# Encoder trunk on one core: the second FFN product in five groups of weight pairs, with its other work placed by a clock kept at build time

## The chip, the cores and the metric

The kernel runs on one core of a Trainium2 chip. The metric is the device time of one execution in microseconds (us), as the median of several runs. A profile is one further execution, taken by the hardware profiler. Engines are named as in the profile: PE (TensorE, matmuls), PEld (its weight loads, which overlap PE), DVE (VectorE), ACT (ScalarE), POOL (GpSimd) and SP (SyncE, whose queue issues nearly all DMAs).

## What is computed

One layer of an encoder trunk on 1280 tokens of width 1024 (1024 of a prompt, 256 of a sample), all in float32: a gated short convolution and a SwiGLU feed-forward network (FFN), each between two RMS norms.

```
def trunk(x, ...):
    h = rms_norm(x, norms[0])
    mix = short_conv_mixer(h, conv_w_in, conv_w, conv_w_out)
    x = x + rms_norm(mix, norms[1])
    h = rms_norm(x, norms[2])
    return x + rms_norm(swiglu(h, ffn_w_in, ffn_w_out), norms[3])

def swiglu(x, w_in, w_out):
    gate, up = jnp.split(x @ w_in, 2, axis=-1)
    return (jax.nn.silu(gate) * up) @ w_out
```

The hidden width of the FFN is 2816, which is 22 blocks of 128 or 11 pairs of blocks. The change is in the last product, `(silu(gate) * up) @ w_out`, and in the norm and residual after it.

## The kernel before

Every float32 operand is split into a high part and a low remainder, and each product is the sum of three matmuls (`TERMS`: high by high, high by low, low by high). Every large product is also done by a seven-product scheme on 2 x 2 blocks (Winograd's form of Strassen's), so that four blocks cost seven products instead of eight. For that, sums and differences of the activations and of the weights have to be made.

**First FFN product** (`ffn_in`, line 852). It runs over the 22 blocks of the hidden width. A class `Block` issues its products on PE; ACT and DVE turn the results into activations `act`. After every second block `spill(j)` (line 765) makes the seven stationary combinations of pair `j` (`A11`, `A12`, `S1` to `S4`, `A22`): for each one ACT copies the high part, DVE subtracts the low part, and two DMAs write both to a scratch tensor `actd` in DRAM. Here the instructions of each engine are ordered by the framework's scheduler.

**Second FFN product** (lines 889 to 1144). From here on the program's own order is kept (`tc.manual_schedule()`, line 1117). Tokens are taken in five units of two 128-token blocks (`UNITS`), the hidden width in six groups of pairs:

```
GROUPS = [[0]] + [[j, j + 1] for j in range(1, KP, 2)]
```

For each group and each unit (`STREAM`, 30 steps) `unit_products` (line 975) issues seven products, each of three matmuls per pair of the group, all from line 990. They go into three PSUM banks `x`, `z` and `y`. After each product the bank is added to a half row of the result `y` in SBUF by DVE (`add`, line 100); in the first group four of the seven are copied by ACT instead (line 106). Bank `x` takes four products one after another without being cleared, bank `z` two: the next product into a bank waits until the sum before it has been read. With the order of lines 1009 to 1028 (`A11` into x, `S1` into z, the unit before's last product, `S2` into x, `S4` into z, `A12` into y, `S3` into x) two other products lie between two uses of bank x.

What else has to be done in this stage:

- **Weights.** For each pair `load_w4` (line 894) issues three DMAs for 1 MB of raw weights (`w4r`), and the generator `w4_steps` (line 903) makes four blocks of it (`b11`, `b22`, `t13`, `t24`): four ACT copies and eight DVE operations (three low parts of 128x1024, one of 128x512, four sums or differences of 128x512). `step` (line 962) does one stage of this; the loop of lines 1129 to 1140 calls it after every second product, provided the pair's load has been issued and there is a place in SBUF.
- **Activations.** `load_units` (line 947) reads the combinations of a unit back from `actd`: per pair one DMA of 768 KB (`ut`, 6 of the 7 combinations), and for the group one of 256 KB (`ut_3l` and the like, the seventh, in pieces of 1 KB).
- **The last spill** (pair 10), stage by stage through the generator `rest`, and **the end**: `finish` (line 1051) takes the squares of a finished row on ACT, the power on POOL, and scales and adds the residual on DVE; for the last unit lines 1067 to 1093 do the same by halves.

SP issues all loads and stores in program order from one queue, and an instruction that waits holds back what stands behind it; the same holds for ACT and DVE.

SBUF has 23 places of 8 KB per partition (`SLOTS`, tags `b`), 3 of tag `a` and 2 of tag `s`, taken and given back at build time by `get` and `put`.

Of the kernel before, what the change touches and what calls it, by code (L numbers as in the profile page):

```python
# [31 lines left out]
GROUPS = [[0]] + [[j, j + 1] for j in range(1, KP, 2)]  # L32
# [4 lines left out]
def encoder_kernel(ctx: ExitStack, tc: tile.TileContext, xT, x, g0T, gB, cwT, w1, w2, w3, w4, out_p, out_s):  # L37
# [723 lines left out]
    A11, A12, S1, S2, S3, S4, A22 = range(7)  # L761
# [3 lines left out]
    def spill(j):  # L765
# [14 lines left out]
        part(A11, a11)  # L780
        yield
        part(A12, a12)
        yield
        part(A22, a22)
        yield
        add(a21, a21, a22)
        yield
        part(S1, a21)
        yield
        sub(a11, a11, a21)  # L790
        yield
        part(S2, a11)
        yield
        add(a22, a22, a11)
        yield
        part(S3, a22)
        yield
        add(a12, a12, a11)
        yield
        part(S4, a12)  # L800
# [47 lines left out]
    def w4_early():  # L848
        while not {0, 1} <= set(made) and step():
            pass  # L850

# [37 lines left out]
    t4, raw4 = {}, {}  # L889

    def pieces():
        return len(free["a"]) + len(free["s"]) - bool(act_left)

    def load_w4():

        j = len(raw4)
        if j < KP and pieces() >= 2:
            raw4[j] = [get(f"w4r{j}{h}", [2, 512], kind="as") for h in (0, 1)]
            nc.sync.dma_start(raw4[j][0], w4[2 * j].rearrange("p (b c) -> p b c", b=2))
            for b in (0, 1):  # L900
                nc.sync.dma_start(raw4[j][1][:, b], w4[2 * j + 1][:, (1 - b) * H : (2 - b) * H])

    def w4_steps():

        for gi, grp in enumerate(GROUPS):
            yield 1, grp[0], gi
            b11 = get(f"w4b11_{gi}", [len(grp), 2, 512], F32R)
            for jn, j in enumerate(grp):
                (ra, rb), t = raw4[j], {"b11": b11[:, jn]}
                copy(t["b11"][:, 0], ra[:, 0])  # L910
                sub(t["b11"][:, 1], ra[:, 0], f32(t["b11"][:, 0]))

                def block(what, src):
                    t[what] = get(f"w4{what}_{j}", [2, 2, 512], F32R)
                    copy(t[what][:, 0], src)

                def low(what, src):
                    sub(t[what][:, 1], src, f32(t[what][:, 0]))

                yield 1, j, gi  # L920
                block("b22", rb)
                low("b22", rb)
                yield 0, j, gi
                sub(ra[:, 0], ra[:, 1], ra[:, 0])
                sub(ra[:, 1], rb[:, 0], ra[:, 1])
                yield 1, j, gi
                block("t13", ra)
                sub(rb[:, 0], ra[:, 0], rb[:, 0])
                add(rb[:, 1], rb[:, 1], rb[:, 0])
                yield 1, j, gi  # L930
                block("t24", rb)
                low("t13", ra)
                yield 0, j, gi
                low("t24", rb)
                put(ra, rb)
                made[j] = t
                yield 0, grp[min(jn + 1, len(grp) - 1)], gi
            t4[gi] = b11

    made = {}  # L940
    w4_gen = w4_steps()
    w4_next = [next(w4_gen)]
# [243 lines left out]
```

## Time and profile before

| | us |
|---|---|
| median of 3 runs | 1297.59 (1297.58 to 1298.13) |
| the profiled execution's own time | 1298.22 |
| its span, first to last instruction | 1296.3 |
| PE busy in the span | 1248.8 (96%) |
| DVE busy | 863.1 (67%) |
| ACT busy | 469.2 (36%) |
| mean granted clock of TensorE | 0.985 of full speed |

Only the last fifth of the span is touched by the change: the second FFN product starts at about 1003 us, its last matmuls start at 1280.7 us, and the rest is norm, residual and output. In the trace a line is often that of a helper (line 100 is every `add`), so tiles tell the work apart: `xo`, `yo`, `zo` are the banks of the second product, `y` the result rows, `w4r` raw weights, `w4b` and `w4t` split weights, `ut` stationary activations. Matmuls are pipelined: the start of the next one tells the pace, not the duration of one.

### The profile page before, as it was taken

The page shows a single profiled execution, that of the slowest core. Times are in us where ns is not written, and L with a number is a line of the kernel's source. Part 1 is how long each engine was busy: PE and PEld are TensorE (multiplying, and loading weights), DVE is VectorE, ACT ScalarE, POOL GpSimd, SP SyncE. Part 2 cuts the span into 40 slices and gives each one's busy share as a digit, 9 for nine tenths or more (in the row PEclk, how much of TensorE's full clock was granted, in tenths as well). Part 3 has the DMA queues.
Part 4 walks back from the last instruction along what each step waited for, and adds up shares of the span by engine and source line. Part 5 has one row for each costly group of instructions (what it writes and reads, how often), then busy time and mean ns, then how long its engine had stood idle before and what let it go on. Part 6 is the DMA issues. An engine that isn't in the chain of part 4 may idle for free.

```text
span 1296.3 us, 15930 instructions
## 1 busy us (share of the span) xinstructions
PE 1248.8 (96%) x6213; PEld 1054.4 (81%) x6213; DVE 863.1 (67%) x1219; ACT 469.2 (36%) x709; POOL 27.7 (2%) x49
## 2 busy tenths in 40 slices
PE   8799999999999989999999999999999999899995
PEld 6588888888778778888888888888888778688874
DVE  7996755747265786566566565565666688677777
ACT  7743333324133553343343343343343521111022
POOL 0100000000011100000000000000000000000001
PEclk9899999999999989999999999999999999899998
DMA  7404031325963214363363452453554678766475
GB/s 260 163 33 146 33 114 65 93 70 166 325 226 111 98 52 130 95 187 115 113 187 97 131 176 94 145 155 99 161 172 154 224 255 277 292 240 260 174 279 228
DMA packets 171738, 207.35 MB, mean 160 GB/s; under 512 B 7696, under 2 KB 135824, under 8 KB 170640
## 3 DMA queue, kind: packets, MB, share of 16 engines
q1 hardware_dynamic: 171232, 205.82, 48.0%
q8 instruction: 48, 0.79, 0.2%
q10 hardware_dynamic: 432, 0.53, 0.1%
q14 instruction: 26, 0.21, 0.0%
HBM read 134.89 MB, written 71.43 MB: 159 GB/s over the span
## 4 chain that ended last, share of the span: by engine, by line
PE 83%; DVE 6%; DMA 6%; ACT 2%; issue 1%; POOL 1%; SPq 1%; POOLq 0%; ACTq 0%
PE xo L990 9%; PE mx L672 5%; PE zo L990 5%; DMA ut<-actd 2%; PE yo L990 2%; DMA w4r<-w 1%; DMA wrf__3029<-w 1%; PE xv__150 L204 1%; DVE y L100 1%; PE xf__3543 L204 1%; PE xf__3760 L204 1%; PE xp__710 L204 1%; PE xf__7627 L204 1%; PE xf__7456 L204 1%; PE xf__7243 L204 1%
## 5 line engine op out<-in xcount | busy, mean ns | idle before, releaser
L672 PE MATMUL mx<-w2s,zs 128*128 128x512 f32 x480 | 111.3, 391 | 2.6 <-DMA zs<-zd 2.6
L672 PEld LDWEIGHTS mx<-w2s,zs 128*128 128x128 f32 x480 | 89.4, 188 | 21.2 <-issue 3.0
L990 PE MATMUL xo<-w4t,ut 128*128 128x512 f32 x330 | 86.5, 396 | 5.8 <-DVE y L100 5.4
L93 ACT ACTIVATE st<-act 128x640 fp32r<-128x640 f32 x77 | 56.8, 737 | 94.8 <-DMA actd<-st 56.5
L100 DVE TENSOR_TENSOR y<-y,xo 128x512 f32<-128x512 f32 x105 | 71.3, 684 | 27.5 <-PE xo L990 26.5
L990 PEld LDWEIGHTS xo<-w4t,ut 128*128 128x128 f32 x330 | 62.3, 190 | 20.5 <-DVE y L100 6.5
L94 DVE TENSOR_TENSOR st<-act,st 128x640 fp32r<-128x640 f32 x77 | 63.2, 821 | 16.2 <-ACT st L93 15.4
L106 ACT ACTIVATE w4t<-w4r 128x1024 fp32r<-128x1024 f32 x22 | 23.3, 1061 | 87.3 <-DVE w4r L97 56.8
L100 DVE TENSOR_TENSOR y<-y,zo 128x512 f32<-128x512 f32 x55 | 37.7, 686 | 25.5 <-PE zo L990 24.2
L990 PE MATMUL xo<-w4b,ut 128*128 128x512 f32 x165 | 44.4, 400 | 4.3 <-DMA ut<-actd 4.3
L990 PE MATMUL zo<-w4b,ut 128*128 128x512 f32 x165 | 42.3, 389 | 0.0
L990 PE MATMUL zo<-w4t,ut 128*128 128x512 f32 x165 | 42.3, 389 | 0.0
L990 PE MATMUL yo<-w4b,ut 128*128 128x512 f32 x165 | 42.3, 389 | 0.0
L106 ACT ACTIVATE w4b<-w4r 128x512 fp32r<-128x512 f32 (+1 forms) x22 | 18.3, 841 | 65.7 <-DMA w4r<-w 28.4
L990 PEld LDWEIGHTS xo<-w4b,ut 128*128 128x128 f32 x165 | 31.4, 193 | 12.9 <-DMA ut<-actd 6.5
L990 PEld LDWEIGHTS zo<-w4t,ut 128*128 128x128 f32 x165 | 31.0, 188 | 6.6
L990 PEld LDWEIGHTS zo<-w4b,ut 128*128 128x128 f32 x165 | 30.9, 188 | 6.6 <-ACT y L106 0.2
L990 PEld LDWEIGHTS yo<-w4b,ut 128*128 128x128 f32 x165 | 31.0, 188 | 6.5
L1045 ACT ACTIVATE j_n<-y 128x512 f32<-128x512 f32 x20 | 12.6, 630 | 54.9 <-DVE y L100 54.7
L97 DVE TENSOR_TENSOR w4b<-w4r,w4b 128x512 fp32r<-128x512 f32 (+1 forms) x22 | 21.0, 955 | 17.2 <-ACT w4b L106 17.0
L414 DVE SCALAR_TENSOR_TENSOR row<-u,cw,row 128x256 f32<-128x256 f32 (+1 forms) x32 | 28.0, 880 | 4.1 <-ACT row L412 3.9
L97 DVE TENSOR_TENSOR w4t<-w4r,w4t 128x1024 fp32r<-128x1024 f32 x22 | 26.8, 1220 | 1.1 <-ACT w4t L106 1.1
(2133 smaller groups left out, 3374.7 us busy)
## 6 DMA issues: line engine op xcount, KB each, us to landing
actd<-st SPq DMA_DIRECT2D x154, 320.0 KB, 2.8
ut<-actd SPq DMA_DIRECT2D x55, 768.0 KB, 6.5
zd<-zst SPq DMA_DIRECT2D x32, 320.0 KB, 3.2
zs<-zd SPq DMA_DIRECT2D x8, 1024.0 KB, 6.6
w4r<-w SPq DMA_DIRECT2D x22, 256.0 KB, 4.4
w4r<-w SPq DMA_DIRECT2D x11, 512.0 KB, 6.3
rows<-x SPq DMA_DIRECT2D x10, 512.0 KB, 3.6
xt<-x SPq DMA_DIRECT2D x10, 512.0 KB, 3.6
```

The source lines that it names most:

```text
L93: nc.scalar.activation(hi, src, AF.Copy)
L94: nc.vector.tensor_tensor(out=lo, in0=src, in1=f32(hi), op=ALU.subtract)
L97: nc.vector.tensor_tensor(out=out, in0=a, in1=b, op=ALU.subtract)
L100: return nc.vector.tensor_tensor(out=out, in0=a, in1=b, op=ALU.add)
L106: nc.scalar.activation(out, a, AF.Copy)
L204: nc.tensor.matmul(out[:, :n], stat(w, k), mov(part, k), start=first and k == 0 and j == 0, stop=last and k == KH - 1 and j == 2, skip_gro ...
L414: nc.vector.scalar_tensor_tensor(out=out, in0=src, scalar=cw[:, j, dd : dd + 1], in1=out, op0=ALU.mult, op1=ALU.add)
L672: nc.tensor.matmul(mx[i][h], zs[i][:, part, k], w2t[k][:, w, h * H : (h + 1) * H], start=k == 0 and j == 0, stop=k == KD - 1 and j == 2,)
L990: nc.tensor.matmul(bank[q], ut[n][:, jn, ap] if c == A22 else ut[n, j][:, c, ap], w[:, wp] if what == "b11" else w[:, wp, b], start=start ...
L1045: nc.scalar.activation(junk, halves(ys[i])[h], AF.Square, accum_out=acc[:, h : h + 1])
```

## The change

It rewrites the second FFN product, lines 889 to 1144, as follows.

- **Groups.** Five in place of six: four of two pairs and a last one of three. Each product is six or nine matmuls; there are 175 sums or copies in place of 210. The number of matmuls stays 1155.
- **A clock at build time.** `clock` holds an assumed time for PE, ACT, DVE and the DMAs. After each product's matmuls `fill` takes operations from generators in `background` (weights, the last spill, the finishing of rows) as long as by this clock they end no later than 0.5 us after the product's result is ready, and only then the product's sum is issued. A weight pair may start only when its load has landed by the same clock (`landing`), and its load is issued up to a whole group ahead.
- **Activations in order of use.** The seven combinations stand in `actd` in the order in which the products use them. Per unit one DMA of 1 MB reads the first four for both pairs; the last three are read by a DMA of 256 KB each, in 1 KB pieces. In the last group it is three tiles and two small ones.
- **The spill** is cut into single operations in the same way (`part`), so that ACT's copy and DVE's subtraction can stand apart.
- **The first weights.** The two pairs of the first group are loaded before the last block of the first FFN product and made during it (`early`).
- **The end.** All rows but the last unit's are finished before the last two products; the last unit's `S3` and then `A12` products come before its `A22`, and row by row the norm follows.

```
-GROUPS = [[0]] + [[j, j + 1] for j in range(1, KP, 2)]
+GROUPS = [[0, 1], [2, 3], [4, 5], [6, 7], [8, 9, 10]]
...
-    A11, A12, S1, S2, S3, S4, A22 = range(7)
+    A11, S1, S2, S4, A12, S3, A22 = range(7)
...
-        def part(c, src):
+        def part(c, src, ready=None):
+            done = yield "act", 0.75, ready, 0, 1, 0
             st = get(f"st{j}_{c}", [2, HALF], F32R, kind="as" if j == KP - 1 else "s")
-            split(st[:, 0], st[:, 1], src)
+            copy(st[:, 0], src)
+            done = yield "dve", 0.76, done, 0, 0, 0
+            sub(st[:, 1], src, f32(st[:, 0]))
...
+    MM, ADD = 0.227, 0.62
+    clock = {"pe": 0.0, "act": 0.0, "dve": 0.0, "dma": 0.0}
+    def landing(mib):
+        clock["dma"] = max(clock["dma"], clock["pe"]) + 2.8 * mib
+        return clock["dma"] + 4.0
...
+    def advance(entry, limit):
+        gen, (engine, cost, ready, places, rows, gi) = entry
+        if gi > at["group"] + 1 or places and len(free["b"]) < places + keep() or rows and rows_free() < rows:
             return False
...
+        done = max(clock[engine], ready) + cost
+        if done > limit:
             return False
+        clock[engine] = done
...
+    def fill(limit):
+        while True:
+            load_units()
+            load_w4()
+            if not any(advance(entry, limit) for entry in list(background)):
+                return
...
+    def slot(n, name):
...
+        clock["pe"] = max(clock["pe"], ready_bank.get((n, q), 0.0)) + 3 * len(grp) * MM
+        ready = clock["pe"] + 0.15
...
+        fill(ready + 0.5)
...
+        first = gi == 0 and name in ("x1", "z5", "x6", "x4")
+        if first:
+            copy(y, acc)
+        else:
+            add(y, y, acc)
...
+    for f in range(KF - 1):
         ffn_in(f)
+    load_w4()
+    load_w4()
+    ffn_in(KF - 1)
+    early()
...
+            slot(n, "x1")
+            slot(n, "z5")
+            if n:
+                slot(n - 1, "x4")
...
+            slot(n, "x6")
+            slot(n, "z3")
+            if n < END:
+                slot(n, "y2")
...
+                slot(n, "x7")
+        slot(END, "x7")
...
+        norm_right(0)
+        norm_right(1)
+        slot(END, "y2")
+        norm_left(0)
+        scale(0, 0)
+        scale(0, 1)
+        slot(END, "x4")
+        norm_left(1)
+        scale(1, 0)
+        scale(1, 1)
```

Three places show what is moved. The first is DVE around the first operation on weight pair 6 (`w4b11_3<-w4r60`), before the change, where it stands in the second unit after its load; `xo2_1` is bank x of group 2, unit 1.

```order
L94 TENSOR_TENSOR st10_4_8512<-act21_7626,st10_4_8512 128x640
L100 TENSOR_TENSOR y1_7824<-y1_7824,xo2_1_8453 128x512
L97 TENSOR_TENSOR w4t24_5_8501<-w4r51_8336,w4t24_5_8501 128x1024
L100 TENSOR_TENSOR y2_7825<-y2_7825,xo2_2_8525 128x512
L100 TENSOR_TENSOR y2_7825<-y2_7825,zo2_2_8539 128x512
L97 TENSOR_TENSOR w4b11_3_8403<-w4r60_8547,w4b11_3_8403 128x512
L100 TENSOR_TENSOR y1_7824<-y1_7824,xo2_1_8453 128x512
```

And the same operation with the change, at the start of group 2:

```order
L100 TENSOR_TENSOR y4_8141<-y4_8141,yo1_4_8541 128x512
L100 TENSOR_TENSOR y4_8141<-y4_8141,xo1_4_8496 128x512
L97 TENSOR_TENSOR w4b11_3_8563<-w4r60_8308,w4b11_3_8563 128x512
L100 TENSOR_TENSOR y0_7850<-y0_7850,xo2_0_8556 128x512
L97 TENSOR_TENSOR w4b22_6_8565<-w4r61_8309,w4b22_6_8565 128x1024
L100 TENSOR_TENSOR y0_7850<-y0_7850,zo2_0_8569 128x512
L97 TENSOR_TENSOR w4r60_8308<-w4r60_8308 128x512
L100 TENSOR_TENSOR y4_8141<-y4_8141,xo1_4_8496 128x512
```

One operation on weights now stands between every two sums, and the pair belongs to the group that is used next.

The second place is SP's queue around the load of the same pair 6, before (the `ut` loads are those of group 2, units 2 and 3, and `ut4` unit 4):

```order
L956 DMA ut2_2l_8465<-actd_108 128x2x256
L774 DMA actd_108<-st10_4_8512 128x5x128 x2
L954 DMA ut3_3_8533<-actd_108 128x1536
L954 DMA ut3_4_8535<-actd_108 128x1536
L956 DMA ut3_2l_8537<-actd_108 128x2x256
L899 DMA w4r60_8547<-w4 128x1024
L901 DMA w4r61_8548<-w4 128x512 x2
```

and with the change (the number after `ut` and `us` counts the 25 steps, so `ut8` is group 1, unit 3):

```order
L1007 DMA ut7_0_8243<-actd_108 128x2x1024
L1007 DMA us6_4_2_8253<-actd_108 128x2x256
L1007 DMA us6_5_2_8255<-actd_108 128x2x256
L1007 DMA us6_6_2_8257<-actd_108 128x2x256
L1007 DMA ut8_0_8297<-actd_108 128x2x1024
L923 DMA w4r60_8308<-w4 128x1024
L925 DMA w4r61_8309<-w4 128x512 x2
L1007 DMA us7_4_2_8331<-actd_108 128x2x256
```

The load has moved from the group in which the pair is split to the group before it, behind the blocks of a step two ahead; the unit's loads are four in place of three.

The third place is the end of DVE's order, before: `y3` is the unit before the last, `y4` the last.

```order
L100 TENSOR_TENSOR y4_7827<-y4_7827,xo5_4_9705 128x512
L103 TENSOR_TENSOR yg9_9773<-y4_7827,g3_9387 128x512
L1081 TENSOR_SCALAR n3r9_9771<-n3e9_9770,n3p9_9772 128x1
L1089 SCALAR_TENSOR_TENSOR y4_7827<-yg8_9765,n3r8_9763,x1l4_9702 128x512
L1089 SCALAR_TENSOR_TENSOR y4_7827<-yg9_9773,n3r9_9771,x1l4_9702 128x512 x2
L1089 SCALAR_TENSOR_TENSOR y4_7827<-yg8_9765,n3r8_9763,x1l4_9702 128x512
L1058 SCALAR_TENSOR_TENSOR y3_7826<-y3_7826,n3_7t_9789,g3_9387 128x1024
L100 TENSOR_TENSOR y3_7826<-y3_7826,x1l3_9617 128x1024
```

With the change:

```order
L100 TENSOR_TENSOR y4_8141<-y4_8141,yo4_4_9748 128x512
L103 TENSOR_TENSOR yg8_9735<-y4_8141,g3_9252 128x512
L1205 TENSOR_SCALAR n3r8_9733<-n3e8_9732,n3p8_9734 128x1
L1214 SCALAR_TENSOR_TENSOR y4_8141<-yg8_9735,n3r8_9733,x1l4_9655 128x512 x2
L100 TENSOR_TENSOR y4_8141<-y4_8141,xo4_4_9658 128x512
L103 TENSOR_TENSOR yg9_9743<-y4_8141,g3_9252 128x512
L1205 TENSOR_SCALAR n3r9_9741<-n3e9_9740,n3p9_9742 128x1
L1214 SCALAR_TENSOR_TENSOR y4_8141<-yg9_9743,n3r9_9741,x1l4_9655 128x512 x2
```

The two 128x1024 operations on `y3` no longer stand last, and row 8 is scaled and sent before the last sum of row 9.

## Rows read from the trace of the kernel before

**Rows 1.** The page's head: span, and PE's busy time and share.
```profile
span 1296.3 us, 15930 instructions
...
PE 1248.8 (96%) x6213; PEld 1054.4 (81%) x6213; DVE 863.1 (67%) x1219; ACT 469.2 (36%) x709; POOL 27.7 (2%) x49
```
**Rows 2.** PE in order of time, second product: start, us, instruction, count [idle before].
```profile
1002.96 0.84 PE L990 MATMUL xo<-w4b,ut 128*128 128x512 f32 x3
...
1029.78 1.52 PE L990 MATMUL xo<-w4b,ut 128*128 128x512 f32 x6
1031.14 1.52 PE L990 MATMUL zo<-w4t,ut 128*128 128x512 f32 x6
...
1057.57 1.65 PE L990 MATMUL xo<-w4t,ut 128*128 128x512 f32 x6 [1.11 <-DVE y L100]
...
1104.11 1.52 PE L990 MATMUL yo<-w4b,ut 128*128 128x512 f32 x6
1109.94 2.93 PE L990 MATMUL xo<-w4t,ut 128*128 128x512 f32 x6 [4.30 <-DVE y L100]
...
1115.02 1.53 PE L990 MATMUL zo<-w4t,ut 128*128 128x512 f32 x6
...
1260.84 0.96 PE L990 MATMUL xo<-w4b,ut 128*128 128x512 f32 x3 [1.34 <-DMA ut<-actd]
...
1280.69 1.66 PE L990 MATMUL xo<-w4t,ut_5l 128*128 128x512 f32 x6
```
**Rows 3.** Windows of 20 us: engines' busy us (instructions), clock, DMA share, GB/s.
```profile
1100.00:1120.00 20.00, 15.70 (x59) 12.44 (x58) 12.36 (x19) 4.54 (x5) 0.00 (x0) 0.83 0.62 216
1120.00:1140.00 20.00, 18.43 (x80) 14.63 (x79) 11.72 (x16) 1.70 (x2) 0.00 (x0) 1.00 1.02 390
1160.00:1180.00 20.00, 20.00 (x90) 16.54 (x89) 15.46 (x23) 2.12 (x2) 0.00 (x0) 1.00 0.41 152
```
**Rows 4.** The chain of waits in order of time: start, us, what.
```profile
972.84 2.75 PE xf__7456 L204 x12
...
983.75 2.72 PE xf__7627 L204 x12
...
1100.02 7.29 DMA w4r<-w
1107.33 0.64 ACT w4b L106
1108.00 0.69 DVE w4b L97
```
**Rows 5.** Groups of instructions by form, 1000 to 1297: busy, mean ns.
```profile
L100 DVE TENSOR_TENSOR y<-y,xo 128x512 f32<-128x512 f32 x105 | 71.3, 684 | 27.5 <-PE xo L990 26.5
...
L97 DVE TENSOR_TENSOR w4t<-w4r,w4t 128x1024 fp32r<-128x1024 f32 x18 | 21.9, 1219 | 0.0
...
L97 DVE TENSOR_TENSOR w4r<-w4r,w4r 128x512 f32<-128x512 f32 x18 | 12.4, 690 | 0.3
```
**Rows 6.** DMA issues, 1000 to 1290: count, KB each, median us to landing.
```profile
ut<-actd SPq DMA_DIRECT2D x53, 768.0 KB, 6.6
...
w4r<-w SPq DMA_DIRECT2D x8, 512.0 KB, 6.8
...
ut_3l<-actd SPq DMA_DIRECT2D x5, 256.0 KB, 7.8
...
out_s<-y ACTq DMA_DIRECT2D x2, 256.0 KB, 2.1
```
**Rows 7.** All engines but PE in order of time, the end.
```profile
1284.81 0.68 DVE L100 TENSOR_TENSOR y<-y,xo 128x512 f32<-128x512 f32 x1
...
1287.64 2.08 DVE L1089 SCALAR_TENSOR_TENSOR y<-yg,n3r,x1l 128x512 f32<-128x512 f32 x3 [0.44 <-POOL n3r L1085]
...
1290.95 1.23 DVE L100 TENSOR_TENSOR y<-y,x1l 128x1024 f32<-128x1024 f32 x1
1292.20 0.33 SPq L1061 DMA_DIRECT2D out_p<-y  x1
```

More of the change, by code (lines that the diff above doesn't have):

```diff
@@ L894, in load_w4, with rows_free, weights_left @@
+    def rows_free():
+        return len(free["a"]) + len(free["s"])
+    raw4, landed, made = {}, {}, {}
+    places_left = {}
+    def weights_left():
+        return sum(n for gi, n in places_left.items() if gi <= at["group"] + 1)
     def load_w4():
         j = len(raw4)
[L897 to L901, printed above, removed]
@@ L962, in step @@
[L962 to L975 removed]
+                done2 = yield "act", 1.06, done2, 1, 0, gi
+                t24 = block("t24")
+                copy(t24[:, 0], rb)
+                yield "dve", 1.16, done, 0, 0, gi
@@ L977, in unit_products @@
+    def slot(n, name):
         gi, ui = STREAM[n]
         grp = GROUPS[gi]
-        first, last = gi == 0, gi == len(GROUPS) - 1
-        end = n == len(STREAM) - 1
-        i0, i1 = UNITS[ui]
-        bank = {}
-        def run(q, c, what, b, start, dst, cols, copies):
-            if start:
-                bank[q] = new_ps(f"{q}o{gi}_{ui}")
-            for jn, j in enumerate(grp):
-                w = made[j][what]
-                for m, (wp, ap) in enumerate(TERMS):
-                    nc.tensor.matmul(
-                        bank[q], ut[n][:, jn, ap] if c == A22 else ut[n, j][:, c, ap],
-                        w[:, wp] if what == "b11" else w[:, wp, b],
-                        start=start and jn == 0 and m == 0, stop=jn == len(grp) - 1 and m == 2,
-                        skip_group_check=not start,
-                    )
-            y = ys[dst][:, cols * H : (cols + 1) * H]
-            if first and copies:
-                copy(y, bank[q])
-            else:
-                add(y, y, bank[q])
@@ L1039, in encoder_kernel @@
-    tail = {}
-    finishing = []
-    def squares(acc, i, hs_):
-        for h in hs_:
-            junk = get(f"j_n3_{i}_{h}", [512], kind="as")
-            nc.scalar.activation(junk, halves(ys[i])[h], AF.Square, accum_out=acc[:, h : h + 1])
-            put(junk)
+        q, what, b, c, row, cols = PRODUCTS[name]
+        starts = name in ("x1", "z5", "y2")
+        if starts:
+            bank[n, q] = new_ps(f"{q}o{gi}_{ui}")
+        acc = bank[n, q]
+        for jn, j in enumerate(grp):
+            w = made[j][what][b]
+            for m, (wp, ap) in enumerate(TERMS):
+                nc.tensor.matmul(
+                    acc, stat[n, c, j][:, ap], w[wp],
+                    start=starts and jn == 0 and m == 0, stop=jn == len(grp) - 1 and m == 2,
+                    skip_group_check=not starts,
+                )
@@ new lines, in slot @@
+        clock["pe"] = max(clock["pe"], ready_bank.get((n, q), 0.0)) + 3 * len(grp) * MM
+        ready = clock["pe"] + 0.15
+        if ui == len(UNITS) - 1 and name in ("x1", "y2", "x7", "x4"):
+            for j in grp:
+                put(*made[j]["tiles"][what])
+        if (n, c) in held_ut:
+            put(held_ut.pop((n, c)))
+        fill(ready + 0.5)
+        if ui not in ys:
+            ys[ui] = get(f"y{ui}", [2, D])
+        i = UNITS[ui][row]
+        y = ys[ui][:, row, cols * H : (cols + 1) * H]
@@ L1117, in encoder_kernel @@
+    background.append(w4_entry)
+    pending[0] = early
+    for f in range(KF - 1):
+        ffn_in(f)
+    load_w4()
+    load_w4()
+    ffn_in(KF - 1)
+    early()
+    if not {0, 1} <= set(made):
+        raise RuntimeError("no place for the first weights")
+    begin(spill(KP - 1))
     with tc.manual_schedule():
-        load_units(1)
+        clock.update(pe=0.0, act=1.0, dve=2.0, dma=0.0)
+        LAST = len(GROUPS) - 1
         for n, (gi, ui) in enumerate(STREAM):
-            load_units(n + 1)
-            at[0] = gi
+            at.update(group=gi, unit=n)
```

401 lines of the change are left out of this document (233 added, 168 removed).

## The prediction

> **What bounds the kernel now.** I read the page's head first: PE is busy for 96% of the span [rows 1], so a gain has to come from PE's idle time, or from the end where PE has nothing left. Then PE in order of time over the second FFN product. Undisturbed, six matmuls take 1031.14 - 1029.78 = 1.36 us [rows 2], 0.2267 us each. The product has 5 units x 7 products x 11 pairs x 3 = 1155 matmuls, so 1155 x 0.2267 = 261.8 us. They take from 1002.96 to 1280.69 + 1.36 = 1282.05 [rows 2], which is 279.1 us. **17.3 us are lost inside the stage.** The end is another item: from 1282.05 to the span's end at 1296.3 [rows 1] are **14.2 us** without useful matmuls.
>
> Where the 17.3 us lie, from the starts in rows 2:
>
> - The first group has 34 products of three matmuls (0.68 us) up to 1029.78: 23.1 us of work in 26.8 us, so 3.7 us are lost. A sum takes DVE 0.684 us [rows 5], as long as its product, so nothing else fits between two sums.
> - The wait at 1109.94 is the largest. The product before begins at 1104.11 and needs 1.36 us, so 4.5 us pass; then twelve matmuls take 1115.02 - 1109.94 = 5.1 us in place of 2.7, because the clock is at the lower of its two levels (1.2 in place of 2.4 GHz; the window shows a mean granted clock of 0.83 [rows 3]). Together 6.8 us. The chain of waits says why [rows 4]: the load of a weight pair was issued at 1100.02 and landed 7.29 us later, ACT's copy of it, DVE's subtraction behind that copy, and behind those the sum that PE waited for. DVE had the subtraction in its order before the load could have landed.
> - A short wait for a sum at 1057.57, idle 1.11 us, and four waits for activations (one of them at 1260.84, idle 1.34 us) [rows 2], together some 6 us with what it takes to start again. The rest, below 1 us, is in slivers.
>
> Later groups show the other state: in 1160 to 1180 the trace holds 90 matmuls, a full window at this pace, with DVE busy 15.5 of 20 us [rows 3].
>
> **The change, part by part.**
>
> *Groups.* The matmuls stay 1155, at 261.8 us. DVE loses 35 sums, 35 x 0.684 = 24 us of busy time [rows 5], which counts only where DVE is late. In the first group a product now lasts 1.36 us against a sum of 0.684, so the 3.7 us there go.
>
> *The clock.* DVE's work per group of 47.6 us (210 matmuls): 35 sums x 0.684 = 23.9 us, and per weight pair three operations of 1.22, five of 0.69 [rows 5], 7.1 us: 38 us with two pairs, 45 us in the fourth group with three. It fits, with 5% to spare in the fourth group. Overlap of neighbours helps: three scale operations in a row take 2.08 us [rows 7], 0.69 each, of which each is listed longer. As for lateness, a bank is read again two products later, 2.72 us; take off the sum and 2.0 us are left. After the first group at most one operation of 1.22 us stands ahead of a sum in the new order. So DVE should not stop PE. ACT's copies in the first group (0.6 us) have the same room.
>
> *The loads.* In the new order of SP pair 6 is loaded a group before its first use. The tightest pair is the fourth (pair 3): six products, 8.2 us, lie between its load and its first copy, against a landing of 6.8 [rows 6]. The small activation loads stand eight products, 10.9 us, ahead of their use, against 7.8 us [rows 6]; the 1 MB loads nine products or more, 12 us. So the waits on loads go, and with them the slow clock. What each queue is asked to do: SP's is in order, and a store of the last spill ahead of a load waits for ACT and DVE; those are now placed to the same time as the load, so I cost that at nothing. POOL gets the same powers as before.
>
> *The start of the stage.* ACT now has two weight copies and one spill copy ahead of the first read of the last block's bank x. The second weight load can go out when a place is free, after the product that ends at 972.84 + 2.75 = 975.6 [rows 4]; with 6.8 us to landing [rows 6] and three copies of about 0.64 [rows 4] the read ends at 984.3, and PE wants the bank at 983.75 [rows 4]. So 0 to 0.6 us; I take 0, because that landing is measured in a busier stage.
>
> *The end.* Before: the last sum starts only at 1284.81, 2.8 us after the last matmul, and two operations on another row stand last on DVE; the last DMA is issued at 1292.20 and needs until 1296.3 [rows 7]. With the change the sum of row 8 is ready with one product (9 x 0.2267 = 2.04 us) still to run. From a sum's start to its scaling takes 1287.64 - 1284.81 = 2.83 us [rows 7]: row 8 is scaled from 0.8 us after the last matmul and takes DVE until 2.2 (two of 0.69); then the last sum, 2.83 us, two scalings of 0.69, and 2.1 us until the half row of 256 KB has landed [rows 6]: 2.2 + 2.8 + 1.4 + 2.1 = 8.5 us, in place of 14.2. **Gain 5.7 us.**
>
> *What is left over.* The waits that stay are not in the trace. Their bounds are 0 (as in 1160 to 1180) and 17.3 us (all of them come back elsewhere). I take 2 us, near the lower end: one short wait for a sum as at 1057.57 and a fraction of one for a load, since the first group is the only one with more of everything than a clean stretch shows.
>
> **Sum**, against the profiled execution's own 1298.2: - 17.3 + 2.0 - 5.7 = 1277.2. The median of the runs lies 0.6 below that execution, so **1276.6 us**.
>
> **The rivals.**
>
> 1. *The DMA engines become the bound in the first group.* Between its first product and the next group's stand, in SP's order, activation loads of five units (9.2 MB), four weight pairs (4.2 MB) and seven spills (4.6 MB): 18 MB in 47.6 us, 378 GB/s. The window at a full DMA share moved 390 GB/s [rows 3], and the spill goes in 512-byte pieces. For it: there is no reserve, a queue must form. Against: the margins are 8 to 12 us and more, and afterwards a step needs 1.8 MB in 9.5 us. Price: seven waits of 1.34 us [rows 2], 9 us, in place of the 2: about 1284. The Trainium skill, Perfetto Trace Analysis, section DMA Optimizations, says that small DMAs (under 2 KB) carry a large overhead per transfer and that batching is better; three of seven combinations are now read in 1 KB pieces, where it was one, and by that rule this rival is likelier. The trace agrees in part: 256 KB in such pieces land in 7.8 us where 768 KB take 6.6 [rows 6], but both stand in the same queue.
> 2. *DVE comes late at each weight pair.* In the packed stretches an operation stands between every two sums, and the assumed times may be short. For it: 45 of 47.6 us in the fourth group. Against: 2.0 us of room at each sum. Price: each of nine pairs costs 1.11 us plus the refill, 1.27 (from 1057.57 against a due 1056.30): 11.4 in place of 2, about 1286.
> 3. *Slower.* What happened once at 1109.94 happens at each pair made in this stage: a copy on ACT, in order, waits for its load, DVE behind it, PE behind DVE. Price: nine times 6.8 = 61 us, so 1277 - 2 + 61 = 1336. It decides from the point where a load lands later than its pair's first copy plus some 2 us, 10 us for the tightest pair, far more for those loaded a group ahead. Against it are 6.8 us [rows 6].
> 4. *The stage does not gain*, because new waits replace the old ones: only the end is won, 1297.6 - 5.7 = 1292.
>
> **How the numbers follow.** The forecast (residual waits of 0 to 6 us, 1274 to 1281) has 0.66, the DMA case 0.14, late DVE 0.12, no gain in the stage 0.05, slower 0.03. Range 1273 to 1287: it takes in the lower bound of no wait at all (1274.6) with a little for the end, and above the first two rivals. 0.2% is 2.6 us, about what a measurement of this kernel can tell from no change. All cases but the slower one lie below 1295; with 0.02 for something between: faster 0.95, same 0.02, slower 0.03.
>
> **What would show it.** Right: PE's starts in the second product 1.36 us apart per six matmuls nearly throughout, about 264 us from the first to the last; no idle time before a matmul above 1.5 us; granted clock 1.00 until the end; the last DMA issued some 6.5 us after the last matmul. The start of the stage stays at 1003 us. Wrong: idle time on loads of activations in the first 60 us of the stage (rival 1), on sums behind `w4t` or `w4b` operations in the fourth group (rival 2), DVE waiting for ACT's copy of a weight pair by several us (rival 3).

## The result, and the profile after

The changed kernel takes **1284.86 us** (median of 4 runs, 1283.68 to 1286.38), the kernel before 1297.86 us beside it (4 runs, 1297.58 to 1298.71): a ratio of 0.9899, 95% interval 0.9882 to 0.9917. It is faster by 1.0%, 13.0 us; 21.0 were forecast.

The page's head of the changed kernel, to be held against [rows 1], with the clock row of its 40 slices:

```profile
span 1284.6 us, 15904 instructions
PE 1246.4 (97%) x6213; PEld 1055.6 (82%) x6213; DVE 840.7 (65%) x1177; ACT 465.4 (36%) x694; POOL 27.0 (2%) x49
...
PEclk9899999999999989999999999999999989999999
```

PE has as many matmuls as before, and DVE is 22.4 us less busy, as the sums that went say (24 by the prediction). In the clock row one slice of the last fifth stands at 8. PE in order of time shows what is there (start, us, instruction, count, idle before it and what ended that); it answers to [rows 2]:

```profile
1003.13 1.52 PE L1131 MATMUL xo<-w4b,ut 128*128 128x512 f32 x6
...
1041.41 1.52 PE L1131 MATMUL zo<-w4t,ut 128*128 128x512 f32 x6
1042.77 1.52 PE L1131 MATMUL xo<-w4t,us 128*128 128x512 f32 x6
1050.79 2.93 PE L1131 MATMUL xo<-w4t,ut 128*128 128x512 f32 x6 [6.50 <-ACT y L106]
1053.51 2.76 PE L1131 MATMUL zo<-w4b,ut 128*128 128x512 f32 x6
...
1057.69 1.52 PE L1131 MATMUL xo<-w4t,us 128*128 128x512 f32 x6
...
1272.93 2.21 PE L1131 MATMUL xo<-w4t,us 128*128 128x512 f32 x9
```

The stage runs from 1003.13 to 1272.93 + 9 x 0.2267 = 1274.97, which is 271.8 us for 261.8 us of matmuls: **10.0 us are lost, where it was 17.3.** Up to 1042.77 stand 29 products, 174 matmuls, 39.4 us of work in 39.6: nothing is lost. Then the product due at 1042.77 + 1.36 = 1044.13 starts at 1050.79, 6.7 us late, and the 18 matmuls from 1050.79 to 1057.69 take 6.9 us in place of 4.1, since after the wait the clock stands at the lower of its two levels (1.2 in place of 2.4 GHz; the mean granted clock is 0.67 from 1043 to 1053). That is 9.5 of the 10.0 us, in **one stall**; all that comes after it, the rest of the first group and four groups, runs at PE's pace.

The releaser is ACT's copy of a product result. ACT in order of time shows what that copy stood behind:

```profile
1033.94 0.73 ACT L106 ACTIVATE st<-act 128x640 fp32r<-128x640 f32 x1
...
1049.51 0.74 ACT L106 ACTIVATE st<-act 128x640 fp32r<-128x640 f32 x1 [11.80 <-DMA actd<-st]
1050.15 0.58 ACT L106 ACTIVATE y<-xo 128x512 f32<-128x512 f32 x1
```

The copy at 1049.51 belongs to the last spill: it writes the high part of `S3` into a row `st`, and that row still held `S2`, whose store to DRAM had not landed. ACT stood still for 11.80 us, and the copy of bank x, whose product had ended when the next began at 1041.41, stood behind it in ACT's order; PE's next product into that bank has to wait until it is copied. By the program's places only one row of five was left to the spill there: two held the raw weights of the fifth pair, two the activations that are being spilled. DVE's and SP's lines say why the store was late (`SPq` is SP's queue; x2 are the two stores, high and low part):

```profile
1034.70 0.82 DVE L97 TENSOR_TENSOR st<-act,st 128x640 fp32r<-128x640 f32 x1 [3.28 <-ACT st L106]
```
```profile
1036.44 1.10 SPq L925 DMA_DIRECT2D w4r<-w  x2
...
1038.12 1.50 SPq L1007 DMA_DIRECT2D us<-actd  x3
1039.67 2.45 SPq L777 DMA_DIRECT2D actd<-st  x2
```

The low part was ready at 1035.5. The stores went out at 1039.67 and 1041.83, behind six loads whose issue began at 1036.44, and landed just before 1049.5, some 7.6 us after the second. That SP's issue began only then has a cause of the same kind, in the view of SP's waits from 1003 to 1051 (us in total, times, longest):

```profile
SPq L925 <- DMA actd<-st: 5.0, 2, 4.2
```

By the program's places the second half of the fifth pair's weights goes into the row that `S1` was in, so SP waited 5.0 us for the store of `S1` to land, and the store of `S2` stood behind that. The kernel's own clock takes a row to be free 4.5 us after its low part is made (`row_free`, `done + 4.5`); it took 14. The windows, to be held against [rows 3] (us, busy us and instructions by engine, clock, DMA share, GB/s), show how full the DMA engines were:

```profile
1013.00:1023.00 10.00, 10.00 (x45) 8.05 (x44) 6.12 (x10) 4.76 (x8) 0.00 (x0) 1.00 0.98 314
1023.00:1033.00 10.00, 10.00 (x45) 8.27 (x45) 8.36 (x11) 4.85 (x8) 0.00 (x0) 1.00 0.90 274
1033.00:1043.00 10.00, 10.00 (x46) 8.26 (x45) 7.50 (x11) 3.89 (x6) 0.00 (x0) 1.00 0.89 291
1043.00:1053.00 10.00, 3.50 (x11) 2.57 (x10) 2.97 (x4) 3.49 (x6) 0.00 (x0) 0.67 0.94 302
```

A share of 0.9 and more, at 274 to 314 GB/s; in [rows 3] a full share moved 390. The chain of waits tells another story at this place, and it misleads:

```profile
1042.16 7.95 DMA ut<-actd
...
1050.15 0.59 ACT y L106
...
1050.79 2.93 PE xo L1131 x6
```

It puts ACT's copy down to an activation load that was issued at 1042.16. But PE was already reading its unit's tile `ut` then (1041.41), so the load belongs to a later unit. And it had not landed at 1042.16 + 7.95 = 1050.11: the view of this load alone (tile `ut`, 1042.1 to 1043) gives 9.8 us from issue to landing, which is 1051.9, after the copy had run.

```profile
DMA to landing us min/median/max: 9.8/9.8/9.8
```

The chain infers what ended a wait from what came last in time, here a part of a load. So the trace itself speaks against the load and for the store, and the experiments put the store to the test.

The groups by form and the DMA issues, 1000 to 1285, answer to [rows 5, 6]: 85 sums of this form in place of 105, at the same duration, and the medians to landing of the new loads.

```profile
L100 DVE TENSOR_TENSOR y<-y,xo 128x512 f32<-128x512 f32 x85 | 58.2, 685 | 28.6 <-PE xo L1131 28.3
```
```profile
ut<-actd SPq DMA_DIRECT2D x17, 1024.0 KB, 7.1
us<-actd SPq DMA_DIRECT2D x60, 256.0 KB, 4.6
```

Last the end, all engines in order of time, to be held against [rows 7]:

```profile
1275.67 1.41 DVE L1214 SCALAR_TENSOR_TENSOR y<-yg,n3r,x1l 128x512 f32<-128x512 f32 x2 [0.65 <-POOL n3r L1209]
...
1277.00 0.68 DVE L100 TENSOR_TENSOR y<-y,xo 128x512 f32<-128x512 f32 x1
...
1279.47 1.42 DVE L1214 SCALAR_TENSOR_TENSOR y<-yg,n3r,x1l 128x512 f32<-128x512 f32 x2 [0.72 <-POOL n3r L1209]
1280.91 0.34 ACTq L1218 DMA_DIRECT2D out_s<-y  x1
```

From 1274.97 to 1284.6 are 9.6 us, where it was 14.2.

### The profile page after: what moved, and what is told of

The parts are those of the page before. It is cut to its first block, busy times and chain, and to the rows that moved or that the text cites. A ratio compares the mean times of both kernels' runs of the same rounds, so it can differ in the third digit from the quotient of the medians.

```text
span 1284.6 us, 15904 instructions
## 1 busy us (share of the span) xinstructions
PE 1246.4 (97%) x6213; PEld 1055.6 (82%) x6213; DVE 840.7 (65%) x1177; ACT 465.4 (36%) x694; POOL 27.0 (2%) x49
## 4 chain that ended last, share of the span: by engine, by line
PE 88%; DVE 6%; DMA 3%; ACT 1%; issue 1%; POOL 1%; SPq 0%; DVEq 0%; POOLq 0%; ACTq 0%
PE xo L1131 11%; PE zo L1131 6%; PE mx L672 5%; PE yo L1131 3%; DMA wrf__3029<-w 1%; PE xv__150 L204 1%; PE xf__3543 L204 1%; PE xf__6682 L204 1%; PE xf__3760 L204 1%; PE xf__7635 L204 1%; PE xf__7456 L204 1%; PE xf__7243 L204 1%; PE xf__7069 L204 1%; PE xf__6856 L204 1%; PE xf__6469 L204 1%
## 5 line engine op out<-in xcount | busy, mean ns | idle before, releaser
L100 DVE TENSOR_TENSOR y<-y,xo 128x512 f32<-128x512 f32 x85 | 58.2, 685 | 28.6 <-PE xo L1131 28.3
L1131 PE MATMUL xo<-w4t,us 128*128 128x512 f32 x273 | 68.9, 389 | 0.0
L1131 PE MATMUL xo<-w4t,ut 128*128 128x512 f32 x222 | 57.0, 397 | 6.5 <-ACT y L106 6.5
L1131 PEld LDWEIGHTS xo<-w4t,us 128*128 128x128 f32 x273 | 51.2, 188 | 10.7
L1131 PEld LDWEIGHTS xo<-w4t,ut 128*128 128x128 f32 x222 | 42.3, 191 | 16.0 <-ACT y L106 6.9
L106 ACT ACTIVATE w4t<-w4r 128x1024 fp32r<-128x1024 f32 (+1 forms) x23 | 23.5, 1023 | 73.1 <-DVE w4r L97 60.2
L100 DVE TENSOR_TENSOR y<-y,zo 128x512 f32<-128x512 f32 x45 | 30.8, 685 | 18.2 <-PE zo L1131 17.9
L1163 ACT ACTIVATE junk<-y 128x1024 f32<-128x1024 f32 (+1 forms) x12 | 11.0, 917 | 75.5 <-DVE y L100 74.2
L1131 PE MATMUL yo<-w4b,us 128*128 128x512 f32 x114 | 29.2, 392 | 0.0
L97 DVE TENSOR_TENSOR w4t<-w4r,w4t 128x1024 fp32r<-128x1024 f32 (+1 forms) x23 | 26.9, 1173 | 0.7 <-ACT w4t L106 0.7
```

Of the source, the lines that this page charges most:

```text
L97: nc.vector.tensor_tensor(out=out, in0=a, in1=b, op=ALU.subtract)
L100: return nc.vector.tensor_tensor(out=out, in0=a, in1=b, op=ALU.add)
L106: nc.scalar.activation(out, a, AF.Copy)
L1131: nc.tensor.matmul(acc, stat[n, c, j][:, ap], w[wp], start=starts and jn == 0 and m == 0, stop=jn == len(grp) - 1 and m == 2, skip_group_c ...
L1163: nc.scalar.activation(junk, src, AF.Square, accum_out=acc[:, col : col + 1])
```

## The experiments

In the profiled executions of all these kernels the stage starts between 999.95 and 1003.79 us, while the 1000 us ahead of it are the same in all of them but for the first weights and the places in `actd`; the unaltered changed kernel alone, profiled twice, starts at 1003.13 and 1001.97. So beside each median stand two lengths: the stage (first matmul to the end of the last) and the end behind it. The changed kernel has 271.8 and 9.6, the kernel before 279.1 and 14.2.

**Is it the row?** Two edits take away the reuse that comes too early, in different ways, and leave every byte to be moved.

```
-            row_free[(free["a"] + free["s"])[-1]] = done + 4.5
+            row_free[(free["a"] + free["s"])[-1]] = done + 14.0
...
-                row_free[tag] = max(row_free.get(tag, 0.0), done + 4.5)
+                row_free[tag] = max(row_free.get(tag, 0.0), done + 14.0)
```

> The changed kernel, with one assumed time altered: a row of the last spill is taken to be free again 14.0 us after its combination is done, in place of 4.5 us; so the copies of the last spill are placed later among ACT's other work. Theory A (a reused row: ACT's spill copy waits for the store of the row's earlier content, ACT's copy of a product result stands behind it in order, and PE behind that): the one long stall of the changed kernel, 6.7 us of waiting and 2.8 us at the lower clock, goes, and nothing comes in its place: 1284.9 - 9.5 = 1275.4 us, between 1274 and 1278. Theory B (the DMA engines are too slow for the first group's bytes): the same bytes move in the same time, so the wait comes back at another place, on an activation load or on a weight load: 1281 to 1286 us.

Measured: 1274.24 us (1273.13 to 1276.48), ratio to before 0.9815, 0.9795 to 0.9835. PE waits for nothing that the trace names in the whole stage; stage 262.2 us, end 9.7. The spill copies now stand at 1015.2, 1023.8, 1040.1 and 1055.7 and wait for no store. The window in which the changed kernel stalled shows DMA engines as full, and PE at work beside them:

```profile
1043.00:1053.00 10.00, 10.00 (x46) 8.27 (x45) 8.78 (x13) 3.62 (x5) 0.00 (x0) 1.00 1.07 379
```

Theory A by its number; theory B, by which the wait comes back elsewhere, falls.

```
-        elif rows_free() >= 2 + bool(act_left):
+        elif rows_free() >= 2 + bool(act_left) and not (j == 4 and act_left):
```

> The changed kernel, but the fifth weight pair's raw weights don't take rows of the spill's kinds while the last spill is unfinished, so the spill turns over three rows or more in place of one; the assumed times stay. Theory A (the single reused row): the stall goes or shrinks to below 3 us, 1275 to 1279 us; the load of the fifth pair comes later, which has a group of slack. Theory B (bytes of the first group): only the order of some bytes changes, 1281 to 1286 us, with a wait of 4 us or more left on some transfer.

Measured: 1275.62 us (1274.13 to 1276.15), ratio 0.9820, 0.9798 to 0.9842; no wait of PE, stage 262.3, end 9.9. With more rows to turn over and the short assumed time of 4.5 us the stall goes as well. So it is the pair of the two, one row and a store that lands later than assumed.

**How much later?** The assumed time was also set between the two values:

```
-            row_free[(free["a"] + free["s"])[-1]] = done + 4.5
+            row_free[(free["a"] + free["s"])[-1]] = done + 9.0
```

(and in the same way two lines further on)

> The changed kernel with rows of the last spill taken to be free after 9.0 us, between 4.5 and 14.0 us. In the changed kernel the row's store landed 14 us after its low part was ready. Theory A (the wait is the landing less the place at which ACT comes to the copy): the spill copies stand some 4 us later in ACT's order, the wait shrinks from 6.5 to 0 to 3 us: 1274 to 1280 us. Rival (the wait goes only when the assumed time is as long as the real one, since the store itself moves back with the copies): a wait of 5 us or more stays, 1283 to 1286 us.

Measured: 1276.36 us (1274.89 to 1277.61), ratio 0.9826, 0.9806 to 0.9846; stage 262.2, end 9.6. One spill copy still waits for a store:

```profile
1048.58 0.74 ACT L106 ACTIVATE st<-act 128x640 fp32r<-128x640 f32 x1 [2.59 <-DMA actd<-st]
```

PE doesn't feel it. The assumed time needn't be the real one: what is left of the wait must only be shorter than what PE can do without ACT.

**Is SP's queue to blame, or the DMA engines?**

```
-                nc.sync.dma_start(
+                (nc.gpsimd if j == KP - 1 else nc.sync).dma_start(
                     actd[:, j, :, (2 * c + p) * P : (2 * c + p + 1) * P].rearrange("u p t -> p u t"),
```

> The changed kernel, with the fourteen stores of the last spill issued from POOL's queue in place of SP's; nothing else moves. In the changed kernel the low part that the store needs was ready at about 1035.5 us, the store was issued by SP at 1039.7 to 1041.8, behind loads, and landed at about 1049.5. Theory A1 (the store is late because SP's queue, in order, holds it up): issued some 4 to 6 us earlier it lands near 1044, the 6.7 us of waiting shrink to 0 to 2 us, and with them the slow clock: 1275 to 1279 us. Theory A2 (the row is late because the DMA engines are full, the queue makes no difference): the landing stays at 1048 to 1050 and the time at 1283 to 1286 us.

Measured: **1289.04 us** (1287.18 to 1289.90), ratio 0.9925, 0.9905 to 0.9944; stage 276.2, end 9.1. Both expectations missed, for the store went out later still (and SP waited 11.8 us with the fifth pair's load for the row of `S1`). POOL in order of time, with the idle time ahead of each store:

```profile
1039.98 0.88 POOL L777 DMA_DIRECT2D actd<-st  x1 [2.51 <-issue]
1046.07 0.88 POOL L777 DMA_DIRECT2D actd<-st  x1 [5.21 <-issue]
```

The low part of `S2` was made by 1034.9 and its store stands at 1046.07. The rows name no releaser for POOL's idle time ("issue"), but the landings tell. This is the store at 1039.98 alone (tile `st`, 1039.9 to 1040.5):

```profile
DMA to landing us min/median/max: 5.8/5.8/5.8
```

It landed at 1045.8, and the next store started 0.3 us later. In this stage the same holds for eight of the eleven stores that follow another in POOL's queue; the other three were not ready sooner. So the run put a queue of another kind in SP's place, one store at a time, and doesn't tell A1 from A2. As a dose it is the clearest of all. Its chain of waits, undisturbed by a load this time, has the whole mechanism:

```profile
1046.07 7.55 DMA actd<-st
...
1053.72 0.74 ACT st L106
1054.45 0.49 ACT y L106
...
1054.99 2.93 PE xo L1131 x6
```

PE's wait grows from 6.5 to 11.3 us, by 4.8, and the median by 1289.04 - 1284.86 = 4.2.

```
-            if n == 0:
+            if gi == 0:
                 ...
```

(the branch reads the last three combinations of a unit as one tile; now in the whole first group)

> The changed kernel, but in the first group the last three combinations of a unit are read by one DMA of 768 KB in pieces of 3 KB in place of three of 256 KB in pieces of 1 KB: the same bytes. Theory B (small pieces make the DMA engines the limit of the first group): the busy share of the DMA engines from 1013 to 1043 us falls from 0.9 to about 0.8, the store of the reused row lands 1 to 3 us earlier and the stall shrinks by as much or goes: 1276 to 1283 us. Theory A1 (the row's store is held up in SP's queue, and small pieces are no matter): the stall stays within 1 us, 1283 to 1286 us. A third reading: one large load takes its places earlier in SBUF and so delays weight loads, which would show as waits behind weight copies and 1286 us or more.

Measured: 1276.21 us (1273.57 to 1276.49), ratio 0.9823, 0.9804 to 0.9843; no wait of PE, stage 262.2, end 9.6. The windows from 1013 to 1043:

```profile
1013.00:1023.00 10.00, 10.00 (x46) 8.29 (x45) 5.75 (x9) 5.00 (x8) 0.00 (x0) 1.00 0.90 327
1023.00:1033.00 10.00, 10.00 (x45) 8.27 (x45) 6.76 (x9) 4.41 (x8) 0.00 (x0) 1.00 0.79 270
1033.00:1043.00 10.00, 10.00 (x46) 8.26 (x45) 7.27 (x11) 5.08 (x9) 0.00 (x0) 1.00 0.99 329
```

Per full share that is 926 / 2.68 = 346 GB/s, where the changed kernel has 879 / 2.77 = 317 and the run with kept rows, with 1 KB pieces too, 1001 / 3.03 = 330: some 5 to 8% less of the DMA engines' time. The Trainium skill, Perfetto Trace Analysis, section DMA Optimizations, says that DMAs under 2 KB carry a significant overhead and that batching them can raise the throughput; the trace agrees in direction, with those 5 to 8%.

That the pieces made the store late isn't shown, though the time is the one that theory B gave. With the larger tiles the build-time clock places other work too: by the program's places the fourth pair's weights hold the two rows here, not the fifth's, so no load waits for the row of `S1`, and the copies of `S2` and `S3` into the one row stand further apart.

```profile
1038.46 0.74 ACT L106 ACTIVATE st<-act 128x640 fp32r<-128x640 f32 x1 [0.91 <-DMA actd<-st]
...
1046.44 0.73 ACT L106 ACTIVATE st<-act 128x640 fp32r<-128x640 f32 x1
```

They are 8.0 us apart, where in the changed kernel ACT came to the copy of `S3` at 1037.7, 3.8 us after that of `S2`. So this run asks for the row later, as late rows do, beside moving the bytes faster. The runs before it have the small pieces and no stall: the pieces aren't enough to make one.

**What is each part of the change worth?**

```
-GROUPS = [[0]] + [[j, j + 1] for j in range(1, KP, 2)]
+GROUPS = [[j, j + 1] for j in range(0, KP - 1, 2)] + [[KP - 1]]
```

> The kernel before, with one line altered: groups of two pairs from the first pair on and the last pair alone, [0,1] to [8,9] and [10], in place of [0] and five of two. No clock, no new order of the activations, no early weights. Theory G (the grouping is what wins the stage): the 3.7 us of the first group go, and with them some of the waits: 1290 to 1294 us. Theory C (the grouping alone is worth nothing without the clock, since the second pair's weights must then be made before the first product, and the weight operations still stand in DVE's order ahead of what has landed): a new stall of 5 to 10 us at the start of the stage in place of the 3.7, the long stall near 1110 us stays or moves: 1297 to 1306 us.

Measured: **1310.26 us** (1309.93 to 1310.88), ratio 1.0098, 1.0081 to 1.0114: slower than before by 13. Theory C has the sign; the time lies above its range, and the place is another. The start of the stage has no stall and the first group is clean, as theory G said. The long stall stays, and in the last group, now of one pair, products are short again and PE waits for sums and for loads over and over; two lines of PE's time order, one for each kind of stall:

```profile
1130.63 2.93 PE L990 MATMUL xo<-w4t,ut 128*128 128x512 f32 x6 [5.31 <-DVE y L100]
...
1273.27 0.97 PE L990 MATMUL xo<-w4b,ut 128*128 128x512 f32 x3 [2.48 <-DMA ut<-actd]
```

From 1260 on some 17 us are lost; the end takes 14.9.

```
-        fill(ready + 0.5)
+        fill(ready + 6.0)
```

> The changed kernel, with one number altered: other work is placed ahead of a sum if by the clock it ends no later than 6.0 us after the product's result is ready, in place of 0.5 us. It asks whether the clock's bound is what keeps sums on time. Theory C: sums now stand behind up to 5.5 us more of other work on DVE, a bank is wanted again 2.7 us after its product, so PE waits for sums by some 2 us at each weight pair and at the spill's operations: nine pairs by 2 to 4 us, 1295 to 1320 us. Rival (the order of loads and early weights alone do it, the bound hardly matters because the work is spread anyway): 1275 to 1288 us.

Measured: **1322.83 us** (1318.32 to 1325.08), ratio 1.0188, 1.0165 to 1.0212. PE waits for sums ten times, 27.2 us in all, and once 5.1 for a copy of ACT; the starts again at the lower clock come on top. One of them:

```profile
1129.83 2.92 PE L1131 MATMUL xo<-w4t,ut 128*128 128x512 f32 x6 [4.22 <-DVE y L100]
```

The same groups, loads and end in program, only placed by a looser bound, and 38 us more: without the tight bound nothing of the gain is left.

```
-GROUPS = [[0, 1], [2, 3], [4, 5], [6, 7], [8, 9, 10]]
+GROUPS = [[0]] + [[j, j + 1] for j in range(1, KP, 2)]
```

(with the tests for groups of two and for the first weights adapted to it)

> The changed kernel with the old six groups ([0], then five of two pairs): the clock, the order of the activations and the new end without the regrouping. My term for the groups was 3.7 us (the first group's 34 short products at DVE's pace). Expected by that term: DVE can't keep up in the first group, 3 to 4 us lost there, and 35 more sums elsewhere hidden. The reused spill row: fewer bytes are read per product in the first group, but it lasts half as long, so whether the stall of 9.5 us stays is open: 1279 us if it goes, 1288 us if it stays.

Measured: 1288.57 us (1287.16 to 1292.86), ratio 0.9934, 0.9913 to 0.9956. The time that was expected if the stall stays, but neither place is the expected one. Stage 271.0, end 16.3. PE through the first group and into the second:

```profile
1008.88 0.84 PE L1131 MATMUL zo<-w4t,ut 128*128 128x512 f32 x3
...
1026.56 0.84 PE L1131 MATMUL xo<-w4t,us 128*128 128x512 f32 x3
1027.24 1.29 PE L1131 MATMUL xo<-w4b,ut 128*128 128x512 f32 x5
1031.06 0.80 PE L1131 MATMUL xo<-w4b,ut 128*128 128x512 f32 x1 [2.52 <-DVE w4b L97]
...
1034.61 1.22 PE L1131 MATMUL zo<-w4t,ut 128*128 128x512 f32 x2 [1.48 <-ACT w4t L106]
```

From 1008.88 to 1026.56 the short products run 0.68 us apart, 78 matmuls in 17.68 us: DVE does keep up with a product of 0.68 us. But then the weights of the second group aren't made, and PE waits for them; between 1027.24 and 1040.64 the 21 matmuls shown lose 8.6 of the stage's 9.2 us, the restart at the lower clock included. At the end the finishing of the earlier rows finds less room beside the last group's sums, and four operations of 1.2 us on DVE stand ahead of the last sums. No spill row holds up PE here.

**A better version, and the changed kernel again.** To the late rows one edit at the end was added: row 8 is scaled behind the last sum, not ahead of it.

```
         norm_left(0)
-        scale(0, 0)
-        scale(0, 1)
         slot(END, "x4")
         norm_left(1)
+        scale(0, 0)
+        scale(0, 1)
```

> The changed kernel with rows taken to be free after 14.0 us (as in the run with late rows) and one more edit at the end: the two scalings of row 8 stand behind the last sum and its norm on DVE, not ahead of them. In the run with e2's edit the last sum started 2.3 us after the last matmul's end because DVE first waited for POOL's power of row 8 and scaled it (1.41 us). Expected: the last sum starts some 0.2 to 0.5 us after the last matmul in place of 2.0 to 2.3, row 8 is scaled while POOL takes the last power, and the last store is issued 1.0 to 1.4 us earlier; the end shrinks from 9.6 to about 8.3 us and the time to about 1273 us. Rival: the four stores of 256 KB now follow each other within 3 us and the last lands later by what it was issued earlier: no gain, 1274.2.

Measured: 1274.71 us (1272.84 to 1275.43), ratio 0.9820, 0.9805 to 0.9834; stage 262.2, end 8.3. The end of this kernel, whose last matmul ends at 1264.87:

```profile
1265.07 0.69 DVE L100 TENSOR_TENSOR y<-y,xo 128x512 f32<-128x512 f32 x1
...
1266.74 2.73 DVE L1214 SCALAR_TENSOR_TENSOR y<-yg,n3r,x1l 128x512 f32<-128x512 f32 x4
1266.97 0.92 POOL L1209 TENSOR_TENSOR n3r<-n3r,nhalf 128x1 f32<-128x1 f32 x1 [1.38 <-DVE n3r L1205]
```

The last sum starts 0.2 us after the last matmul, and in the profiled execution the end is 1.3 us shorter, as expected. The median doesn't show it (1274.71, where the rival gave 1274.2): the run with late rows alone happened to start its stage 2.7 us earlier in its profiled execution, and 1.3 us lie within what the runs of one kernel differ.

> The fastest version so far (rows free after 14.0 us, row 8 scaled behind the last sum) with the 3 KB reads of the first group added. Theory A (only the wait for the reused row costs; the DMA engines' load costs nothing once no wait hangs on it): the stage is already at its matmuls' 261.8 us within 0.5, nothing is left to win, 1272.5 to 1275 us as without this edit. Theory B: the first group still loses something to small pieces, 1 us or more less than without.

The edits are those shown for late rows, for 3 KB reads and for the end. Measured: 1275.04 us (1271.43 to 1277.93), ratio 0.9814, 0.9790 to 0.9839; stage 262.2, end 8.5. As theory A has it: the time is that of the version without the edit within what runs differ, so a gain of 1 us from the larger pieces can't be told from none.

> The changed kernel itself, unaltered, on the same chip as the fastest version, so that the two stand beside each other, and to see whether the stall is there in each execution. Expected: 1284 to 1286 us, with PE's wait near 1050 us of 5 to 7 us again. Rival (the stall is a matter of chance in the DMA queue): another length of the wait by more than 2 us, and a time that moves with it.

Measured: 1283.80 us (1282.14 to 1284.82), ratio 0.9883, 0.9865 to 0.9900; stage 269.7. PE waits 5.63 us at the same product, ACT 10.94 for the same store. So the stall is no accident of one execution, and on the same chip the version before this run (with 3 KB reads, 1275.04) stands 8.8 us below it.

## Why the prediction was right and where it was wrong

The sign, the order of size and the mechanism of the gain were right, and the time lay in the range. In the profiled execution the start is 0.2 us later than assumed, less than two executions of one kernel differ; the stage is 8.0 longer than the 263.8 forecast, and the end 1.1 longer: 1277.2 + 9.3 = 1286.5, against that execution's own 1286.38.

- **The waits of before go.** Right: of the 17.3 us nothing stands at its old place, and every kernel with the five groups, the clock's bound and no row stall has a stage of 262.2 or 262.3 us, 0.4 to 0.5 over its matmuls.
- **Groups.** The 3.7 us went, and the reason given was wrong. I put them down to sums as long as their products. But in the first group ACT copies four of seven results, and the trace before shows the short products at PE's pace from 1018.88 to 1023.64, with DVE idle ahead of the sums there:

```profile
1023.59 0.69 DVE L100 TENSOR_TENSOR y<-y,zo 128x512 f32<-128x512 f32 x1 [3.13 <-PE zo L990]
```

  Either part of the change makes the first group nearly clean, the groups alone and the clock with six groups, and each alone pays elsewhere: some 17 us around the last group of one pair, and 8.6 us until the second group's weights are made. Grouping alone made the kernel slower, so the 3.7 us can't be booked to it apart from the clock.
- **The clock.** Right, and worth more than I wrote: with its bound loosened from 0.5 to 6.0 us the time is 1322.83.
- **The loads.** Right: PE waits for none of them in this stage, in the fourth group as little as elsewhere, where DVE's work was nearest to its limit.
- **The end.** Its steps were right (row 8 scaled from 0.7 us after the last matmul, 0.8 forecast; last store issued 5.9 after it, 6.5 forecast). The term was mis-sized by 1.1 us: I let the end stop when the last half row has landed, but 1.6 us lie between that landing and the span's end, and the old 14.2, taken to the span's end, held such a time. The steps took 0.6 us less than forecast and so hid part of it.
- **What is left over.** This is the step that failed, and it makes nearly the whole of the miss. I took 2 us and had written, in the part on loads, that a store of the last spill ahead of a load waits for ACT and DVE and that "I cost that at nothing". I asked who waits in front of the store, never who waits behind it for its row: ACT with the next spill copy, SP with a load of weights. The term measured 10.0 us, 9.5 of them from one reused row. The number needed stood in the code beside the trace: 4.5 us assumed for a row, and landings of 6.6 to 7.8 us in [rows 6] before any wait in SP's queue.
- **The rivals.** The first came within 1 us of the result, 1284, which is luck, for its mechanism didn't happen: not one activation load made PE wait, in place of seven, and the kernels with late rows and with kept rows, which move the same bytes in the same pieces, have no stall. Its premise held in part: the first group's DMA engines were at a share of 0.9 and more, but a full share moves 317 to 330 GB/s there, not the 390 of [rows 3], and of the 378 GB/s asked for 276 came in the changed kernel (1003 to 1051) and 302 in the run with kept rows, without a wait of PE in the latter. A full queue became dear only through a row that was wanted back. The other rivals didn't happen: no sum was late behind weight work, no weight copy waited where PE felt it, and the stage did gain.

What stays open: how much of the store's 14 us is SP's order and how much the DMA engines. The store was ready 4 us before its first issue and landed some 7.6 us after the second, which is a split by the trace; the run that was to separate them added a delay of its own, and the one with 3 KB reads moved the copies as well. The 4 us go back to SP's wait for the row of `S1` by the order of its queue, which is argued and not tried by itself: the run with late rows has a wait of 5.4 us at the same load and no stall.

## What to carry to other kernels

When an order is fixed at build time, look for buffers that are written again after a store: the copy that refills one waits for the landing, and on an in-order engine everything behind it waits too. Price the reuse with the landing that the busy stretch shows and with the issue's place in its queue, and spread it over more buffers before looking for faster transfers. The same holds for a load into such a row: it holds back its whole queue. A chain of waits infers its releaser from what came last in time; if that has no part in the operation, look up when it landed, and read the engine's own order instead.

## What was not expected of the hardware

Stores issued from POOL's queue went out one at a time: eight of the eleven that follow another in this stage started 0.3 us after the store ahead of them had landed, 2.5 to 6.7 us after POOL's last instruction, the store of `S2` as shown above. The two of `S2` were 6.1 us apart, where SP issued them within 2.45 us, and the second left 4.2 us later than from SP. The Trainium skill, DMA: Bandwidth & Descriptors, section Issuing engines are not separate DMA queues, says that issuing from several engines saves only the time it takes to initiate a DMA; here it cost time. What makes POOL wait for the landing no run here shows.
